# Fourth conv tile ahead of keys and queries, and 64-row score products on two halves of the array

## The chip, the cores and the metric

The kernel runs on one core of a Trainium2 chip. The metric is the device time of one execution in microseconds (us). Its engines work side by side, each through its own list of instructions in order: TensorE (PE: matrix products; PEld: loading the stationary operand), VectorE (DVE), ScalarE (ACT), GpSimd (POOL) and SyncE (SP, which here only issues transfers). They wait for one another through semaphores. A program (the tile framework's scheduler) turns the code below into those lists: it takes the order of the code as a priority, but puts an instruction later or earlier where it expects an operand or a buffer to be late.

## The reference

Two layers, each on 512 positions of 1024 features: a feed-forward block, a mixer and a second feed-forward block. The change is in the mixer.

```python
h = rms_norm(x, mix_norm[l])
a, g, q, k, v = jnp.split(h @ w_in[l], splits, axis=-1)
conv_out = conv_module(a, g, conv_w[l], conv_b[l], conv_norm[l])   # GLU, causal depthwise conv (31 taps), norm, swish
q = rms_norm(q.reshape(B, S, H, 2, d).transpose(0, 2, 3, 1, 4), q_norm[l])   # H = 4 heads, 2 maps, d = 64
k = rms_norm(k.reshape(B, S, H, 2, d).transpose(0, 2, 3, 1, 4), k_norm[l])
...
s = jnp.einsum("bhmqd,bhmkd->bhmqk", qi, k) * scale + bias      # blocks of 128 queries, causal
p = jax.nn.softmax(s, axis=-1)
a = p[:, :, 0] - lam * p[:, :, 1]                               # difference of the head's two maps
o = jnp.einsum("bhqk,bhkd->bhqd", a, v)
...
x = x + jnp.concatenate([conv_out, diff_out], axis=-1) @ w_out[l]
```

## The kernel before

Activations are kept with features on the 128 partitions. The large products are made three times over, with a high and a low part of each operand (`mm3`, L158 to L164). The high part of a weight chunk comes from ScalarE (L97), the low part from VectorE or GpSimd (L98); `chunk` (L100) loads and splits one, and its `eng` says who makes the low part. Chunks live in rings of four or five buffers, so a new one waits for an old one to be used up.

`mixer` (L530) does, in the order of its code from L777 on:

- `conv_in(c)` (L537): for conv tile c of four, the products for the gated linear unit (48 matmuls, `ps_pair`), then VectorE and ScalarE make `u` (L557 to L563). The low parts for c = 3 come from GpSimd. The first two tiles are worked together, with the row norms among them.
- `project(which, pair)` (L574): keys (1) and queries (0), two of the four position tiles a call, 48 matmuls (L585 to L587), then the sums of squares (L593, L594), the power on GpSimd (`rsqrt`, L209) and the scaled `qn` (L600). `to_features` (L620) transposes `qn` on TensorE (L624); ScalarE copies the result to `kt`, or twice to `qz`: `qz[:, m]` holds the queries of map m with zeros in the other map's 64 rows, because the factor `gq[:, m]` is zero there (L512 to L517).
- `project_values(j)` (L606): V for one position tile, 24 matmuls (`ps_v`).
- `conv_taps(c, n)` (L646): the 31 taps of a tile. GpSimd adds the first n, with products made by ScalarE (L656, L657); VectorE does the others in one PSUM bank (tag `y`, one buffer, L664 to L669). `POOL_TAPS` gives n for each tile: all 31 for tile 0, none for 1 and 2, ten for 3. For tile 3 VectorE adds GpSimd's sum at the end (L673). `conv_finish` (L678) norms over the four tiles and writes `ch`, `cl` (L687, L688).
- `attend(n)` (L767): step n of 16 (4 query blocks from the last, 4 heads each, so heads of width 512, 384, 256 and 128). `softmaxes` (L694) makes the score product of each map (L703) into a bank of tag `sc` (map 0) or `po` (map 1), two banks each. VectorE adds the bias and takes the minimum (L707, here all signs are turned), ScalarE makes the exponential and its sum (L711). VectorE then makes a factor `c` (L714, L716) and the difference of the maps `e0` (L717). Two steps later `keys_first` (L720) transposes it, a step after that `values` (L729) multiplies by V (L733), and `block_out` (L756) transposes the block's output (L760) and splits it.
- The output projection (L804 to L814): half 0 takes the conv tiles, then half 1 the attention blocks 2 and 3, then 0 and 1; its banks are `sc` and `po` too.

The conv, key and query products also use the banks `sc`, `po` and `mm` in turn (`turn_tag`, L309), so a conv tile that is moved moves them all by one.

Of the kernel before, what the change touches and what calls it, by code (L numbers as in the profile page):

```python
# [11 lines left out]
F32 = mybir.dt.float32  # L12
F32R = mybir.dt.float32r
I32 = mybir.dt.int32
AF = mybir.ActivationFunctionType
ALU = mybir.AluOpType
AX = mybir.AxisListType

P = 128
DEPTH = 2  # L20
SEQ = 512
# [8 lines left out]
TAPS = 31  # L30
# [18 lines left out]

POOL_TAPS = (TAPS, 0, 0, 10)  # L50

# [16 lines left out]
def trunk(ctx: ExitStack, tc: tile.TileContext, xt, par, lamv, relb, onehot,  # L68
# [133 lines left out]
    def col(l, name, i=0):  # L202
        c = _AT[name] + i
        return pars[l][:, c : c + 1]
# [291 lines left out]
    def make_scalars():  # L496
        for l in range(DEPTH):
# [13 lines left out]
            nlam.append(nl)  # L511
            g = const.tile([P, 2], F32, tag=f"gq{l}", name=f"gq{l}")  # L512
            G.memset(g, 0.0)
            for m in range(2):
                d = slice(m * HD, (m + 1) * HD)
                G.tensor_tensor(g[d, m : m + 1], col(l, "q_norm")[d], col(l, "k_norm")[d], op=ALU.mult)
            G.tensor_scalar(g, g, -math.sqrt(HD), None, op0=ALU.mult)  # L517
# [12 lines left out]
    def mixer(l, pr, after):  # L530
        with tc.tile_pool(name="mix", bufs=1) as mp, tc.tile_pool(name="mt", bufs=2) as mt:
# [36 lines left out]

            qz = mp.tile([P, 2, HEADS, SEQ], F32, tag="qz", name="qz")
            kt = mp.tile([P, HEADS, SEQ], F32, tag="kt", name="kt")  # L570
# [49 lines left out]
            def to_features(which, pair):  # L620
                for j in (2 * pair, 2 * pair + 1):
# [5 lines left out]
                    if which == 1:  # L627
                        S.activation(kt[:, :, t], pt, AF.Copy)
                    else:
                        for m in range(2):  # L630
                            S.activation(qz[:, m, :, t], pt, AF.Copy, scale=gq[l][:, m : m + 1])

# [61 lines left out]
            def softmaxes(i, h):  # L694
# [7 lines left out]
                for m in range(2):  # L702
                    T.matmul(scs[m], qz[:, m, h, tq], kt[:, h, :W], start=True, stop=True)  # L703

# [10 lines left out]
                c2 = small.tile([P, 1], F32, tag="c2", name="c2")  # L715
                V.tensor_scalar(c2, r2, nlam[l], sm[:, 0, h : h + 1], op0=ALU.mult, op1=ALU.mult)  # L716
                V.scalar_tensor_tensor(e0, scs[1], c2, e0, op0=ALU.mult, op1=ALU.add)  # L717
# [58 lines left out]

            for c in range(CT - 1):  # L777
                conv_in(c)
# [6 lines left out]
            to_features(0, 0)  # L785
            conv_in(CT - 1)
            to_features(0, 1)
            bias = mp.tile([P, HEADS, SEQ], F32, tag="bias", name="bias")
            nc.sync.dma_start(bias, skew[0])
            row["bias"] = bias  # L790

            for n in range(2):
                attend(n)
                project_values(NT - 1 - 2 * n)
                project_values(NT - 2 - 2 * n)
            for c in range(CT):
# [124 lines left out]
```

## Time and profile before

| what | value |
|---|---|
| median of 3 runs | 1797.92 us (1797.81 to 1798.19) |
| the profiled execution | 1798.12 us |
| its span in the profile | 1796.4 us |
| busy: TensorE, its loads, VectorE | 1785.4, 1590.2, 1215.1 us |
| busy: ScalarE, GpSimd | 895.9, 654.5 us |
| start of the first and the last score pass in the first layer | 460.0 and 511.6 us from the span's start |

A row of a group gives line, engine, operation, result and operands, shapes and count, then busy time and mean length of one in ns, then idle time of the engine ahead of it. A row of the timeline gives start and length in us, engine, line, operation, operands and count; in brackets stands how long the engine sat idle before it and what ended that. A matmul's record begins while the one before is still streaming, so lengths overlap, and the time that one takes from the engine is read from start to start. A row of a stretch gives its bounds, its length and the busy time with instruction count of PE, PEld, DVE, ACT and POOL, then the granted TensorE clock, the DMA share and GB/s.

### The profile page before, as it was taken

The numbers are of one execution on the slowest core, as the hardware profiler recorded it, in microseconds if no ns is written. First come the engines' busy times: TensorE is split into PE (matmuls) and PEld (weight loads), VectorE is DVE, ScalarE is ACT, GpSimd is POOL, SyncE is SP. The second block draws the span as 40 slices with busy tenths as digits, with TensorE's granted clock in tenths as the row PEclk, the third lists the DMA queues.
The fourth block names the chain that finished last, engine by engine and source line by source line (L and its number), as shares of the span: only waits on it lengthen the run. The fifth ranks groups of instructions, "written<-read, shape, count | busy, mean of one in ns | idle before, by whom it ended". The sixth has DMA issues, their size and how long they took to land.

```text
span 1796.4 us, 28354 instructions
## 1 busy us (share of the span) xinstructions
PE 1785.4 (99%) x10845; PEld 1590.2 (89%) x10845; DVE 1215.1 (68%) x1862; ACT 895.9 (50%) x1482; POOL 654.5 (36%) x460
## 2 busy tenths in 40 slices
PE   9999999999999999999999999999999999999999
PEld 6899899888778899899888998998887888998997
DVE  7977477569867867477476764765788587673762
ACT  5555255445854446256433543654558354552651
POOL 4242232269843133132112312412797331322420
PEclk9999999999999999999999999999999999999999
DMA  7466476333212366466333664663231133664651
GB/s 242 104 167 197 100 178 187 107 105 94 71 48 83 94 164 179 115 170 184 110 94 95 171 169 115 179 182 118 71 113 52 48 106 89 168 178 112 178 151 59
DMA packets 111721, 231.24 MB, mean 129 GB/s; under 512 B 12151, under 2 KB 33414, under 8 KB 111584
## 3 DMA queue, kind: packets, MB, share of 16 engines
q1 hardware_dynamic: 91488, 191.93, 33.2%
q0 software_dynamic: 19808, 37.33, 12.7%
q8 instruction: 85, 1.39, 0.3%
q14 instruction: 52, 0.43, 0.1%
q10 hardware_dynamic: 288, 0.16, 0.0%
HBM read 227.26 MB, written 3.42 MB: 128 GB/s over the span
## 4 chain that ended last, share of the span: by engine, by line
PE 95%; DVE 2%; issue 1%; ACT 1%; ACTq 0%; DVEq 0%
PE ps_pair L373 38%; PE ps_d L160 9%; PE ps_d L164 9%; PE ps_d L163 9%; PE ps_pair L164 5%; PE ps_pair L163 5%; PE ps_pair L160 5%; PE ps_pair L585 2%; PE ps_pair L586 2%; PE ps_pair L587 2%; PE ps_out L163 1%; PE ps_out L160 1%; PE ps_sc L703 1%; PE ps_out L164 1%; DVE actl L258 1%; PE ps_v L617 1%
## 5 line engine op out<-in xcount | busy, mean ns | idle before, releaser
L97 ACT ACTIVATE whi<-wraw 128x512 fp32r<-128x512 f32 (+2 forms) x600 | 466.2, 801 | 616.4 <-PE ps_pair L373 225.7
L98 DVE TENSOR_TENSOR wlo<-wraw,whi 128x512 fp32r<-128x512 f32 (+2 forms) x556 | 527.4, 971 | 210.1 <-ACT whi L97 205.0
L373 PE MATMUL ps_pair<-acth,wlo 128*128 128x256 f32 x1088 | 307.9, 283 | 0.0
L373 PE MATMUL ps_pair<-actl,whi 128*128 128x256 f32 x1088 | 307.9, 283 | 0.0
L373 PE MATMUL ps_pair<-acth,whi 128*128 128x256 f32 x1088 | 307.9, 283 | 0.0
L163 PE MATMUL ps_d<-hl,whi 128*128 128x512 f32 x704 | 273.9, 389 | 0.0
L164 PE MATMUL ps_d<-hh,wlo 128*128 128x512 f32 x704 | 273.0, 389 | 0.0
L160 PE MATMUL ps_d<-hh,whi 128*128 128x512 f32 x704 | 268.4, 389 | 0.0
L373 PE MATMUL ps_pair<-th,wlo 128*128 128x256 f32 x816 | 230.9, 283 | 0.0
L373 PE MATMUL ps_pair<-tl,whi 128*128 128x256 f32 x816 | 230.8, 283 | 0.0
L373 PE MATMUL ps_pair<-th,whi 128*128 128x256 f32 x816 | 230.8, 283 | 0.0
L143 POOL TENSOR_TENSOR wraw<-wraw 128x512 f32<-128x512 f32 x68 | 104.1, 1531 | 345.5 <-DMA wraw<-in_gu 293.0
L138 POOL DMA_DIRECT2D wraw<-in_gu x68 | 82.0, 1206 | 384.1 <-DMA wraw<-in_gu 228.0
L373 PEld LDWEIGHTS ps_pair<-actl,whi 128*128 128x128 f32 x1088 | 208.9, 192 | 0.3
L373 PEld LDWEIGHTS ps_pair<-acth,whi 128*128 128x128 f32 x1088 | 208.9, 192 | 0.3
L373 PEld LDWEIGHTS ps_pair<-acth,wlo 128*128 128x128 f32 x1088 | 208.9, 192 | 0.0
L469 DVE SCALAR_TENSOR_TENSOR x<-ps_d,x 128x512 f32<-128x512 f32 x96 | 64.7, 688 | 179.1 <-PE ps_d L164 178.8
L164 PE MATMUL ps_pair<-acth,wlo 128*128 128x512 f32 x448 | 174.5, 391 | 1.1 <-DVE wlo L98 1.1
L163 PE MATMUL ps_pair<-actl,whi 128*128 128x512 f32 x448 | 174.6, 391 | 0.6 <-DVE actl L258 0.3
L160 PE MATMUL ps_pair<-acth,whi 128*128 128x512 f32 x448 | 174.5, 394 | 0.2
L373 PEld LDWEIGHTS ps_pair<-tl,whi 128*128 128x128 f32 x816 | 156.5, 192 | 0.7
L373 PEld LDWEIGHTS ps_pair<-th,whi 128*128 128x128 f32 x816 | 156.5, 192 | 0.6
(174 smaller groups left out, 3268.8 us busy)
## 6 DMA issues: line engine op xcount, KB each, us to landing
wraw<-in_gu SPq DMA_DIRECT2D x208, 256.0 KB, 4.0
wraw<-in_gu SPq DMA_DIRECT2D x104, 512.0 KB, 3.7
wraw<-in_gu POOLq DMA_DIRECT2D x68, 512.0 KB, 5.8
wraw<-in_wqkv SPq DMA_DIRECT2D x24, 512.0 KB, 3.6
wraw<-in_dn SPq DMA_DIRECT2D x84, 128.0 KB, 3.0
wraw<-in_dn SPq DMA_DIRECT2D x32, 256.0 KB, 3.1
wraw<-in_wag SPq DMA_DIRECT2D x16, 512.0 KB, 3.6
wraw<-in_wout SPq DMA_DIRECT2D x16, 512.0 KB, 3.6
```

What stands on the lines that cost most here:

```text
L97: S.activation(hi, raw, AF.Copy)
L98: (eng or V).tensor_tensor(out=lo, in0=raw, in1=f32(hi), op=ALU.subtract)
L138: nc.gpsimd.dma_start(two.rearrange("p (b c) -> p b c", b=2), u[:, h[0]].unsqueeze(1).broadcast_to([P, 2, 512]), accum_op=ALU.add)
L143: G.tensor_tensor(more[:, h[0]], two[:, h[1]], whole[:, h[0]], op=ALU.add)
L160: first = T.matmul(ps, wh, xh, start=start, stop=False)
L163: T.matmul(ps, wh, xl, start=False, stop=False)
L164: T.matmul(ps, wl, xh, start=False, stop=stop)
L373: mm = T.matmul(ps, l, r, start=first and i == j == 0, stop=False, skip_group_check=True)
L469: V.scalar_tensor_tensor(x[:, m, :], ps, 0.5, x[:, m, :], op0=ALU.mult, op1=ALU.add)
L585: T.matmul(ps[n], xh[:, t], wh, start=k == 0, stop=False)
L586: T.matmul(ps[n], xh[:, t], wl, start=False, stop=False)
L587: T.matmul(ps[n], xl[:, t], wh, start=False, stop=k == KT - 1)
```

## The change

The query copy with zeros goes: `qt` holds the queries once, with one factor for all 128 rows, and each score product takes the 64 rows of its map from `qt` and `kt`. So map 0 lies on the first half of TensorE's rows and map 1 on the second. The fourth conv tile is projected with the other three, ahead of keys and queries. Two V tiles stand ahead of the last `to_features`, and the first two steps of `attend` among the other two. GpSimd takes 6 taps of the fourth tile instead of 10. The factor `c` is made by another instruction with the same operands.

```diff
-POOL_TAPS = (TAPS, 0, 0, 10)
+POOL_TAPS = (TAPS, 0, 0, 6)
...
-            g = const.tile([P, 2], F32, tag=f"gq{l}", name=f"gq{l}")
-            G.memset(g, 0.0)
-            for m in range(2):
-                d = slice(m * HD, (m + 1) * HD)
-                G.tensor_tensor(g[d, m : m + 1], col(l, "q_norm")[d], col(l, "k_norm")[d], op=ALU.mult)
+            g = const.tile([P, 1], F32, tag=f"gq{l}", name=f"gq{l}")
+            G.tensor_tensor(g, col(l, "q_norm"), col(l, "k_norm"), op=ALU.mult)
             G.tensor_scalar(g, g, -math.sqrt(HD), None, op0=ALU.mult)
...
-            qz = mp.tile([P, 2, HEADS, SEQ], F32, tag="qz", name="qz")
+            qt = mp.tile([P, HEADS, SEQ], F32, tag="qt", name="qt")
...
-                        for m in range(2):
-                            S.activation(qz[:, m, :, t], pt, AF.Copy, scale=gq[l][:, m : m + 1])
+                        S.activation(qt[:, :, t], pt, AF.Copy, scale=gq[l])
...
                 for m in range(2):
-                    T.matmul(scs[m], qz[:, m, h, tq], kt[:, h, :W], start=True, stop=True)
+                    half = slice(m * HD, (m + 1) * HD)
+                    T.matmul(scs[m], qt[half, h, tq], kt[half, h, :W], start=True, stop=True)
...
-                V.tensor_scalar(c2, r2, nlam[l], sm[:, 0, h : h + 1], op0=ALU.mult, op1=ALU.mult)
+                V.scalar_tensor_tensor(c2, r2, nlam[l], sm[:, 0, h : h + 1], op0=ALU.mult, op1=ALU.mult)
...
-            for c in range(CT - 1):
+            for c in range(CT):
                 conv_in(c)
             project(1, 0)
             project(1, 1)
...
             project(0, 1)
             to_features(0, 0)
-            conv_in(CT - 1)
-            to_features(0, 1)
             bias = mp.tile([P, HEADS, SEQ], F32, tag="bias", name="bias")
             nc.sync.dma_start(bias, skew[0])
             row["bias"] = bias

-            for n in range(2):
-                attend(n)
-                project_values(NT - 1 - 2 * n)
-                project_values(NT - 2 - 2 * n)
+            project_values(NT - 1)
+            project_values(NT - 2)
+            to_features(0, 1)
+            attend(0)
+            project_values(NT - 3)
+            attend(1)
+            project_values(NT - 4)
             for c in range(CT):
                 conv_taps(c, POOL_TAPS[c])
```

## The prediction

> **What bounds the kernel now.** I read the page first: span, busy shares and the chain that ended last. Then the busy time in stretches of the first layer's attention, then the score products by shape, then the order of single instructions on TensorE and VectorE.
>
> ```profile
> span 1796.4 us, 28354 instructions
> PE 95%; DVE 2%; issue 1%; ACT 1%; ACTq 0%; DVEq 0%
> 474.00:490.30 16.30, 15.87 (x83) 11.02 (x81) 11.69 (x39) 14.23 (x34) 13.81 (x10) 1.00 0.45 131
> 490.30:503.62 13.32, 11.77 (x80) 9.72 (x80) 13.08 (x52) 10.68 (x35) 7.84 (x8) 1.00 0.00 0
> 503.62:515.20 11.58, 11.32 (x60) 8.74 (x61) 11.58 (x35) 9.01 (x26) 2.90 (x5) 1.00 0.01 1
> ```
>
> The chain that ended last lies on TensorE for 95% of the span. So what counts is TensorE work taken away or added and TensorE waits opened or closed. The columns of the stretches are length, then busy time of TensorE, its weight loads, VectorE, ScalarE and GpSimd, then granted clock (1.00 throughout), DMA share and GB/s. In the first stretch TensorE is nearly full. In the second VectorE is (13.08 of 13.32 us) and TensorE is not, in the third both are. The change lies in this stage, which stands twice in the program, once a layer. There TensorE and VectorE are nearly balanced, so work taken from TensorE is only worth what VectorE lets through.
>
> **What the score products cost.** A product of head and map goes through TensorE as two passes. One layer has 16 heads' worth (4 query blocks of 4 heads, here h0 to h15) with two maps (m0, m1), so 64 passes:
>
> ```profile
> L703 PE MATMUL ps_sc<-kt,qz 128*128 128x512 f32 x16 | 7.5, 592 | 0.0
> L703 PE MATMUL ps_sc<-kt,qz 128*128 128x384 f32 x16 | 6.2, 487 | 0.0
> L703 PE MATMUL ps_sc<-kt,qz 128*128 128x256 f32 x16 | 4.6, 382 | 0.0
> ...
> 474.36 0.39 PE L617 MATMUL ps_v<-whi,actl 128*128 128x512 f32 x1
> 474.59 1.88 PE L703 MATMUL ps_sc<-kt,qz 128*128 128x512 f32 x4
> 476.30 0.60 PE L724 MATMUL ps_at<-ident,e 128*128 128x128 f32 x4
> 476.74 2.53 PE L703 MATMUL ps_sc<-kt,qz 128*128 128x512 f32 x6
> ...
> 481.73 1.05 PE L733 MATMUL ps_o<-vv,at 128*128 128x128 f32 x8
> 482.62 0.81 PE L703 MATMUL ps_sc<-kt,qz 128*128 128x384 f32 x2
> ```
>
> Durations overlap in the pipeline, so I take starts. Four 512-wide passes take 476.30 - 474.59 = 1.71 us, 0.427 each; scaled with width, 16 x 0.427 x (1 + 3/4 + 1/2 + 1/4) = 17.1 us a layer. Transposes take 0.44/4 = 0.11 us, value passes 0.89/8 = 0.11 us.
>
> **Edit 1, half-height products.** Each product keeps its columns and its two passes; only its rows are halved. It gains if passes on the two halves run side by side, which needs an m0 and an m1 next to each other in TensorE's order, both ready. The order of the changed program has this at the start of a layer (h0m0 h0m1 h1m0 h1m1). After that come h2m0 h3m0 h4m0 h5m0, then single m1 products with transposes and value passes between, in 16 groups a layer. Only eight passes stand in alternation. If the second pass of one half runs beside the first of the other, 8 spans become 5, a gain of 3 x 0.427 = 1.3 us. Four joints between narrower products give at most 0.5 more. Bounds on TensorE: 0 to -1.8 us a layer; I take -1.3. Of that only what someone waits for reaches the end: in this start a full product takes 0.85 us where VectorE, by the rows below, needs 0.61 for it, so three gaps of 0.24 close, -0.7 us.
>
> The opposite bound is the cost of going between full and partial array. The trace has that in the bias product (33 rows), beside the full-height product of the row factors:
>
> ```profile
> 42.58 0.39 PE L164 MATMUL ps_pair<-acth,wlo 128*128 128x512 f32 x1
> 42.90 0.09 PEld L486 LDWEIGHTS ps_bias<-oneh,relb 33*4 33x4 f32 x2 [0.35 <-issue]
> 42.90 1.02 PE L486 MATMUL ps_bias<-oneh,relb 33*4 33x512 f32 x2
> 43.85 0.19 PEld L160 LDWEIGHTS ps_pair<-acth,whi 128*128 128x128 f32 x1 [0.86 <-issue]
> 43.85 0.50 PE L160 MATMUL ps_pair<-acth,whi 128*128 128x512 f32 x1
> 44.18 0.39 PE L163 MATMUL ps_pair<-actl,whi 128*128 128x512 f32 x1
> ...
> 371.92 0.40 PE L164 MATMUL ps_pair<-acth,wlo 128*128 128x512 f32 x1
> 372.16 1.02 PE L240 MATMUL ps_spread<-diag,ones 128*128 128x512 f32 x2
> 372.61 0.79 PE L160 MATMUL ps_pair<-acth,whi 128*128 128x512 f32 x1
> 373.24 0.40 PE L163 MATMUL ps_pair<-actl,whi 128*128 128x512 f32 x1
> ```
>
> From the L164 ahead to the second matmul behind, the partial product takes 44.18 - 42.58 = 1.60 us and the full one, with as many passes of 512 columns, 373.24 - 371.92 = 1.32. The weights of the partial one were loaded only at 42.90, when the product before was ending, and the load behind it likewise. So in and out cost 0.28 us together. Sixteen groups would be 4.5 us a layer if all lay on TensorE's path; the other bound is 0, where TensorE waits anyway. Thirteen groups (3.6 us) lie before the output projection, where the sum below leaves TensorE waiting: I take 0 for them. Three lie inside the projection, where it has work: 3 x 0.28 = 0.8 us.
>
> [...]
>
> **Edit 2, the order.** In the old program h0 and h1 are scored inside the V projection, so their softmax runs on VectorE while TensorE has V products. In the new one the fourth conv tile stands ahead of K and Q, and all four V tiles stand ahead of the first score. The work ahead is the same, so the first score starts 8 x 0.427 = 3.4 us earlier than 474.59, at 471.2. But all 16 heads then follow with nothing to fill in. VectorE:
>
> ```profile
> 452.99 7.09 DVE L669 SCALAR_TENSOR_TENSOR ps_y<-u,par,ps_y 128x512 f32<-128x512 f32 x9
> ...
> 464.23 0.70 DVE L707 CUSTOM_DVE_ANT_0 ps_sc<-ps_sc,bias 128x512 f32<-128x512 f32 x1
> 464.84 0.75 DVE L669 SCALAR_TENSOR_TENSOR ps_y<-u,par,ps_y 128x512 f32<-128x512 f32 x1
> ...
> 466.29 0.27 DVE L716 TENSOR_SCALAR c<-r,nlam,sums 128x1 f32<-128x1 f32 x1
> 466.47 0.74 DVE L669 SCALAR_TENSOR_TENSOR ps_y<-u,par,ps_y 128x512 f32<-128x512 f32 x1
> 467.13 0.74 DVE L717 SCALAR_TENSOR_TENSOR e<-ps_sc,c,e 128x512 f32<-128x512 f32 x1
> 467.79 0.15 DVE L714 RECIPROCAL r<-sums 128x1 f32<-128x1 f32 x1
> 467.86 0.73 DVE L669 SCALAR_TENSOR_TENSOR ps_y<-u,par,ps_y 128x512 f32<-128x512 f32 x1
> ...
> 475.65 0.69 DVE L707 CUSTOM_DVE_ANT_0 e<-ps_sc,bias 128x512 f32<-128x512 f32 x1 [2.52 <-PE ps_sc L703]
> ...
> 512.27 0.74 DVE L688 SCALAR_TENSOR_TENSOR actl<-u,ghalf,acth 128x512 fp32r<-128x512 f32 x1
> ```
>
> A 512-wide head costs VectorE 2 x 0.61 (464.84 - 464.23) + 0.07 (467.86 - 467.79) + 0.18 (466.47 - 466.29) + 0.66 (467.79 - 467.13) = 2.13 us; by width I estimate 1.3 for 256 and 0.9 for 128. From its first product of h2 (475.65) to the low part of the fourth conv tile (512.27) it needs 36.6 us, waits included, with 12 whole heads between (two of 512, four each of 384 and 256, two of 128). In the new order the same instruction stands behind 11 whole heads (four, four, three, none): +2 x 2.13 - 1.3 - 2 x 0.9 = +1.2 us. The new form of c is an instruction like
>
> ```profile
> L740 DVE SCALAR_TENSOR_TENSOR se<-sums x8: 132/154/164, 480.0 to 1398.7; 128x4 f32<-128x4 f32 x8
> ```
>
> 0.15 for 0.27 us, 11 x 0.12 = -1.3. So again 36.5 us, from 471.2 + 0.9 (first product) = 472.1: the fourth tile's low part starts at 508.6 instead of 512.27. VectorE has four more taps at 7.09/9 = 0.79 us, 3.2 us, but they come before the first score. All taps end near 469 by the old rows, so about 3 us of slack hide them; without it they would be 3.2 us on the path.
>
> TensorE's first output product stands in the new order behind the transposes of block 2, whose input VectorE writes 1.2 us (0.60 for itself, the rest small ones) before that fourth tile: start about 507.4. TensorE's own work from 471.2 to there (26 score products 16.6, 34 transposes 3.7, 68 value passes 7.5, row sums, spread and output transposes 2.3) is 30.1 us, to 501.3. With all thirteen switches it would be 504.9, still before 507.4: VectorE sets this time.
>
> ```profile
> 503.62 0.50 PE L160 MATMUL ps_out<-acth,whi 128*128 128x512 f32 x1 [1.26 <-ACT acth L687]
> ...
> 531.31 0.28 PE L160 MATMUL ps_out<-acth,whi 128*128 128x256 f32 x1
> ```
>
> In the old kernel that first half of the projection lasts from 503.62 to 531.31, 27.7 us, with some 1.5 us of waits for conv tiles. In the new one all tiles are nearly there: 96 x 0.227 = 21.8, left-over heads 3.6, switches 0.8 and 0.5 of waits, 26.7 us, to 534.1. That is 534.1 - 531.3 = **+2.8 us a layer**.
>
> **The rest.** GpSimd loses four tap additions, ScalarE four tap products and four of its eight copies of queries a layer:
>
> ```profile
> 486.47 1.27 POOL L657 TENSOR_TENSOR yp<-yp,prod 128x512 f32<-128x512 f32 x1 [0.20 <-ACT prod L656]
> L631 ACT ACTIVATE qz<-ps_pair,gq 128x512 f32<-128x512 f32 x8 | 4.8, 690 | 3.1 <-PE ps_pair L624 3.1
> ```
>
> The last tap would end at 487.7 - 4 x 1.27 = 482.7. The add that waits for it now stands on VectorE after three heads, at about 472.1 + 3 x 2.13 + 4 products of h3 to h5 (2.2) + waits 1.5 = 482.2. So this gain is used up, and if GpSimd is later every microsecond stalls all softmax behind it: 0 to +2 us, I take +0.3. The four copies lie beside V products: 0 now, a gain of some 2.4 us if TensorE had to wait for them. The moved weight loads keep their count; the bias load passes ahead of all key loads on the SP queue, whose splits start over ten microseconds later than before: 0.
>
> **The sum.** A layer: +2.8 (order, with the switches in the projection) + 0.3 (late tap) - 0.7 (first products side by side) = +2.4; two layers **+4.8 us** on 1798.12 us, the profiled execution (span 1796.4 and 1.7 around it; the median of the runs is 1797.92): **1802.9 us**. Bounds a layer: downwards VectorE's waits gone (some 3.2 us between its rows from 475.65 to 512.27), no switch paid (0.8), no late tap (0.3) and the joints gained (0.5), 2.4 - 4.8 = -2.4; upwards a tap late by 2 us (+1.7), the other 13 switches on the path (+3.6) and nothing side by side (+0.7), +8.4. For two layers 1793 to 1815.
>
> **The rivals.**
> 1. *The halves run side by side and the conv part, three heads earlier in VectorE's order, closes the waits* (the other side). For it: all conv tiles lie ready when the projection starts, and both engines have waits in the old stretches. Against it: groups of one map, and a VectorE that is full from 490 on. By the lower bound 1793. It decides if VectorE's gaps between first score and fourth conv tile come to under 1 us. Chance 0.17. Complete halving of the 17.1 us on the path would be 8.5 us less in each layer, 1781; the order keeps the maps apart, so I hold 0.03 for that.
> 2. *Nothing measurable.* V and conv change places, the scores cost what they did, and the waits that open at the start of the scores are those that close in the projection: 1798, within 3.6 us (0.2%, about what a measurement of this kernel can tell from no change). For it: VectorE needs 36.5 against 36.6 us. Chance 0.2.
> 3. *Switches and the late tap on the path*: 2.4 + 1.7 + 3.6 = +7.7 a layer, 1813. It decides if VectorE waits for scores whose weights were loaded only when the product before had ended. Against it: TensorE has 2.5 us to spare with all of them. Chance 0.1.
>
> My forecast, VectorE setting the start of the projection some 4 us later than before, has 0.5, most of it above 1801.5, where slower by 0.2% begins. So slower 0.1 + 0.45 = 0.55, same 0.2 + 0.05 = 0.25, faster 0.17 + 0.03 = 0.2. The range is 1792 to 1811; out of it lie halving, the upper half of rival 3 and little else. The forecast's own is 1800 to 1807.
>
> **What would show it.** Right: in the stretch from first score to first output product TensorE is busy markedly below the old share and VectorE near full, V products end before the first score, and the output product starts about 4 us later. Partial products show weight loads not overlapped with what is before. Wrong: score passes of m0 and m1 with the same start in many groups, or a TensorE wait inside K, Q or V for a low part from GpSimd. That I count as 0:
>
> ```profile
> 376.23 2.41 POOL L98 TENSOR_TENSOR wlo<-wraw,whi 128x1024 fp32r<-128x1024 f32 x1 [9.39 <-ACT whi L97]
> ```
>
> At 2.41 us a split and 1.27 a tap its new order, followed through by hand from 376.23, has the last V split ready near 454.4, and its first use on TensorE falls near 457.3; the others have 2 to 5 us too.

## The result, and the profile after

The changed kernel takes 1823.6 us (median of 4 runs, 1819.1 to 1824.9) against 1797.9 for the kernel before (1797.7 to 1798.2): ratio 1.0139, 95% interval 1.0126 to 1.0151, so +25.7 us where +4.8 was forecast. The profiled execution took 1822.8 us, and the rows below are of that one.

Three lines of its page: span, granted TensorE clock in 40 slices, and the chain that ended last.

```profile
span 1820.8 us, 28323 instructions
PEclk9999999999999999999999999999997999999999
PE 95%; DVE 3%; issue 1%; DVEq 0%
```

The chain reads much as before. What is new is a 7 among the nines of the clock line, in the attention of the second layer. Busy time by stretch shows what it is (length, then busy time of TensorE, weight loads, VectorE, ScalarE, GpSimd, then granted clock, DMA share, GB/s). Four rows follow the second layer's attention, the last belongs to the first layer:

```profile
1369.50:1375.70 6.20, 5.91 (x18) 2.00 (x18) 4.93 (x17) 6.20 (x15) 6.20 (x4) 1.00 0.29 91
1375.70:1396.20 20.50, 20.50 (x58) 12.31 (x58) 12.43 (x35) 8.27 (x23) 6.65 (x5) 0.50 0.24 75
1396.20:1413.20 17.00, 15.53 (x84) 10.34 (x84) 14.51 (x44) 12.80 (x36) 5.63 (x6) 1.00 0.00 1
1413.20:1420.10 6.90, 6.67 (x23) 5.35 (x24) 6.33 (x23) 4.57 (x14) 1.21 (x2) 0.51 0.00 0
508.70:512.10 3.40, 3.31 (x13) 2.73 (x13) 3.37 (x14) 2.45 (x7) 0.00 (x0) 0.50 0.02 5
```

For 20.5 us the clock is at 0.50. TensorE is full there and VectorE, which should set the pace, works only 12.43 us. Two shorter falls follow the later heads, one in each layer. Read more finely, the falls last 3.41, 20.48 and 6.83 us: one, six and two times 3.41. They start at 508.70, 1375.69 and 1413.24, and the distances are whole multiples of it too, 254 and 11 times 3.413. Half of their 30.7 us is lost where TensorE has work, at most 15.4 us.

The landmarks on TensorE in the first layer (the second row is the weight load of the fifth score product), and two of the second:

```profile
471.21 7.18 PE L700 MATMUL ps_sc<-kt,qt 64*128 64x512 f32 x18
473.12 0.29 PEld L700 LDWEIGHTS ps_sc<-kt,qt 64*128 64x128 f32 x2 [0.76 <-DVE mn L704]
511.14 0.77 PE L160 MATMUL ps_out<-acth,whi 128*128 128x512 f32 x1
561.48 0.40 PE L160 MATMUL ps_pair<-acth,whi 128*128 128x512 f32 x1
1369.54 8.01 PE L700 MATMUL ps_sc<-kt,qt 64*128 64x512 f32 x18
1418.20 0.77 PE L160 MATMUL ps_out<-acth,whi 128*128 128x512 f32 x1
```

The first score starts at 471.21 (forecast 471.2). The first output product starts 39.9 us later (forecast 36.2), and in the second layer 48.7 us later. The row at 561.48 is the first product after the mixer; in the kernel before it was this one:

```profile
554.77 0.40 PE L160 MATMUL ps_pair<-acth,whi 128*128 128x512 f32 x1
```

So the first layer loses 6.7 us, and most of the rest is lost in the second.

GpSimd and VectorE in the first layer, from the timeline:

```profile
473.56 6.98 POOL L98 TENSOR_TENSOR wlo<-wraw,whi 128x1024 fp32r<-128x1024 f32 x3
480.51 1.26 POOL L653 TENSOR_TENSOR yp<-yp,prod 128x512 f32<-128x512 f32 x1
...
472.37 0.69 DVE L704 CUSTOM_DVE_ANT_0 e<-ps_sc,bias 128x512 f32<-128x512 f32 x1 [2.16 <-PE ps_sc L700]
...
477.32 0.94 DVE L713 SCALAR_TENSOR_TENSOR c<-r,nlam,sums 128x1 f32<-128x1 f32 x1
...
478.96 1.61 DVE L737 SCALAR_TENSOR_TENSOR se<-sums 128x4 f32<-128x4 f32 x1
480.49 0.69 DVE L704 CUSTOM_DVE_ANT_0 ps_sc<-ps_sc,bias 128x512 f32<-128x512 f32 x1
...
482.72 0.21 DVE L713 SCALAR_TENSOR_TENSOR c<-r,nlam,sums 128x1 f32<-128x1 f32 x1
...
483.91 0.67 DVE L669 TENSOR_TENSOR u<-ps_y,yp 128x512 f32<-128x512 f32 x1
...
509.99 0.74 DVE L684 SCALAR_TENSOR_TENSOR actl<-u,ghalf,acth 128x512 fp32r<-128x512 f32 x1
```

An operation on one number a row takes 0.94 us, one on four 1.61. GpSimd's three splits of 2.33 us end near 475.9, 478.2 and 480.5; c ends at 478.26 and se at 480.57. Both stand still until the running GpSimd instruction ends, while a 512-wide product that starts beside the last tap takes its usual 0.69.

### The profile page after: what moved, and what is told of

Its sections match the earlier page's. It is cut to its first block, busy times and chain, and to the rows that moved or that the text cites. A ratio compares the mean times of both kernels' runs of the same rounds, so it can differ in the third digit from the quotient of the medians.

```text
span 1820.8 us, 28323 instructions
## 1 busy us (share of the span) xinstructions
PE 1807.7 (99%) x10845; PEld 1596.3 (88%) x10845; DVE 1235.3 (68%) x1870; ACT 888.4 (49%) x1466; POOL 649.8 (36%) x448
## 3 DMA queue, kind: packets, MB, share of 16 engines
HBM read 227.26 MB, written 3.42 MB: 127 GB/s over the span
## 4 chain that ended last, share of the span: by engine, by line
PE 95%; DVE 3%; issue 1%; DVEq 0%
PE ps_pair L373 38%; PE ps_d L164 9%; PE ps_d L163 9%; PE ps_d L160 9%; PE ps_pair L163 5%; PE ps_pair L164 5%; PE ps_pair L160 5%; PE ps_pair L583 2%; PE ps_pair L582 2%; PE ps_pair L584 2%; PE ps_out L160 1%; PE ps_out L164 1%; PE ps_out L163 1%; PE ps_sc L700 1%; PE ps_v L612 1%; PE ps_v L613 1%
## 5 line engine op out<-in xcount | busy, mean ns | idle before, releaser
L98 DVE TENSOR_TENSOR wlo<-wraw,whi 128x512 fp32r<-128x512 f32 (+2 forms) x556 | 534.6, 983 | 200.1 <-ACT whi L97 194.9
L143 POOL TENSOR_TENSOR wraw<-wraw 128x512 f32<-128x512 f32 x68 | 113.0, 1661 | 347.1 <-DMA wraw<-in_gu 299.4
```

The source lines that it names most:

```text
L98: (eng or V).tensor_tensor(out=lo, in0=raw, in1=f32(hi), op=ALU.subtract)
L143: G.tensor_tensor(more[:, h[0]], two[:, h[1]], whole[:, h[0]], op=ALU.add)
```

## The experiments

The change has four parts: the order of the stages (O), six taps instead of ten on GpSimd (T), the new form of c (C), half-height products with queries kept once (H). The table gathers the runs that combine them. Each was timed beside the kernel before.

```
parts       us       ratio and 95% interval
none        1797.9
C           1799.0   1.0005 (0.9995 to 1.0014)
H           1800.1   1.0010 (1.0001 to 1.0019)
O           1803.5   1.0031 (1.0020 to 1.0043)
O H         1804.9   1.0038 (1.0025 to 1.0052)
O T         1806.5   1.0045 (1.0028 to 1.0062)
O T C       1811.9   1.0079 (1.0064 to 1.0094)
O T H       1812.0   1.0078 (1.0063 to 1.0093)
O T C H     1823.6   1.0139 (1.0126 to 1.0151)
```

One way through it: O +5.6, T +3.0, C +5.4, H +11.7, together 25.7. But C alone costs 1.2 and on top of O, T and H 11.6; H alone costs 2.0, on top of O 1.4, of O and T 5.5, of O, T and C 11.7. The parts do not add up; they share something.

**Full height again** (O T C):

```
-    T.matmul(scs[m], qt[half, h, tq], kt[half, h, :W], ...)
+    T.matmul(scs[m], qz[:, m, h, tq], kt[:, h, :W], ...)      # qz zero-padded, as before
```

> The changed kernel with its score products at full height again, queries zero-padded for each map as before; order of the stages, taps and the form of c as changed. Theory A, half-height passes count as less work for what grants TensorE its clock, and this took the clock from 1.00 to 0.50 for 3.4 us in the first layer and 27 us in the second: here the clock is 1.00 in both attention stretches, and the time falls from 1823.6 to 1800 to 1807 us. Rival B, the new order leaves TensorE waiting for VectorE and those waits take the clock down: the stretches at 0.50 stay, 1815 to 1825 us.

Measured: 1811.9 us (1810.0 to 1816.5), mean clock 1.00 in the profiled execution and 0.998 in the three others. The second layer:

```profile
1368.00:1374.20 6.20, 6.16 (x15) 2.38 (x13) 4.32 (x13) 6.20 (x14) 6.20 (x4) 1.00 0.30 85
1374.20:1395.00 20.80, 18.85 (x106) 13.52 (x106) 20.00 (x55) 13.56 (x38) 11.79 (x10) 1.00 0.27 77
```

At the same place, with the same order, TensorE now gets 106 instructions done in 20.8 us where it got 58, and VectorE is busy for 20.00. So the long fall belongs to the half-height products. But the time came out above the 1800 to 1807 expected, and the clock can't be the whole reason: the profiled execution took 1810.0 us, 12 more than the kernel before, without any fall. So order, taps and c lose time at full clock too. One place for it shows in this trace, ahead of the output projection. (`ov` is the output of query block 2, which VectorE writes and TensorE then transposes.)

```profile
508.20 0.68 DVE L748 TENSOR_TENSOR ov<-ps_o,rs_y 128x512 f32<-128x512 f32 x1
509.27 0.73 DVE L688 SCALAR_TENSOR_TENSOR actl<-u,ghalf,acth 128x512 fp32r<-128x512 f32 x1
...
508.94 0.66 PE L760 MATMUL ps_o<-ident,ov 128*128 128x128 f32 x4 [1.51 <-DVE ov L748]
...
510.65 0.71 PE L733 MATMUL ps_o<-vv,at 128*128 128x128 f32 x4 [0.61 <-ACT at L726]
511.12 0.47 PE L160 MATMUL ps_out<-acth,whi 128*128 128x512 f32 x1
```

VectorE writes `ov` 1.07 us ahead of the fourth conv tile (1.2 forecast). But the first output product doesn't follow at once: TensorE still does the transposes and another head's products, with a wait for ScalarE between, and starts it 2.92 us behind the start of `ov`.

**The old form of c** (O T H), and **both** (O T):

```
-    V.scalar_tensor_tensor(c2, r2, nlam[l], sm[:, 0, h : h + 1], op0=ALU.mult, op1=ALU.mult)
+    V.tensor_scalar(c2, r2, nlam[l], sm[:, 0, h : h + 1], op0=ALU.mult, op1=ALU.mult)
```

> The changed kernel with c in its old form (tensor with two scalars) only. Theory lock: the new form of c, with both its inputs in SBUF, stands still until GpSimd's running instruction ends (0.94, 1.02 us where GpSimd is busy, 0.21 where it is not); in the old form every c is back at 0.26 to 0.27, VectorE's way from the first score to the first output product is some 1.5 us shorter in a layer, and the time falls by 2 to 4 us, to 1819 to 1822, if the stretches at half clock stay. Rival: c is not on the path, within 1 us of 1823.6. Theory A: the mean clock stays under 1.00; rival B the same.

> The changed kernel with full-height score products and the old form of c: of the change only the order and six taps instead of ten remain. Theory A with the forecast's account of the order (+2.4 us a layer, of which 0.8 was for switches that are gone and -0.7 for halves side by side): clock 1.00, 1799 to 1804 us. Rival B (order takes the clock down): 1815 us or more with stretches at 0.50.

Measured: 1812.0 and 1806.5 us, mean clock 0.994 and 0.997. The first gain, 11.6 us, was much more than the 2 to 4 expected. The second lies above its 1799 to 1804, and here neither theory holds in its first form: all products are of full height, and the clock still falls, late in the attention:

```profile
503.20:506.61 3.41, 1.77 (x11) 1.15 (x11) 3.41 (x13) 3.41 (x10) 0.00 (x0) 1.00 0.02 5
506.61:513.44 6.83, 6.30 (x21) 5.04 (x20) 4.01 (x18) 2.38 (x11) 0.00 (x0) 0.50 0.00 0
```

In the 3.41 us ahead of that fall TensorE had work for 1.77 us by its records, which overlap; VectorE was full. VectorE's first product and the low part of the fourth conv tile in the same run:

```profile
471.52 0.69 DVE L707 CUSTOM_DVE_ANT_0 e<-ps_sc,bias 128x512 f32<-128x512 f32 x1 [1.95 <-PE ps_sc L703]
...
507.28 0.74 DVE L688 SCALAR_TENSOR_TENSOR actl<-u,ghalf,acth 128x512 fp32r<-128x512 f32 x1
```

Those 35.8 us are what the forecast took as 36.5. The first output product, though, starts only at 509.30, 2.0 us behind the fourth tile, where the forecast had it 1.2 ahead, and the first product after the mixer at 559.48, 4.7 us later than in the kernel before. Now look at the stretch ahead of the long fall in the changed kernel, all engines and then TensorE's instructions that touch it, by shape:

```profile
1372.28:1375.69 3.41, 3.12 (x8) 1.01 (x8) 3.34 (x13) 3.41 (x12) 3.41 (x2) 1.00 0.34 130
```

```profile
L700 PE MATMUL ps_sc<-kt,qt 64*128 64x512 f32 x4 | 2.8, 750 | 0.1
L700 PE MATMUL ps_sc<-kt,qt 64*128 64x384 f32 x4 | 1.8, 535 | 0.2
```

TensorE looks busy (3.12 of 3.41), but with half-height passes alone. This suggests one rule for both: the work in a stretch of 3.41 us counts, and half-height work counts for less, in my sums for half. Here is the lowest stretch of the kernel before (counted back in steps of 3.413 from its one fall, at 1795.03, where its TensorE work is done), which kept its clock, and the one ahead of the changed kernel's fall in the first layer:

```profile
501.36:504.77 3.41, 2.06 (x13) 1.47 (x13) 3.41 (x11) 2.82 (x11) 3.33 (x4) 1.00 0.02 5
505.29:508.70 3.41, 2.02 (x11) 1.31 (x10) 3.41 (x11) 2.99 (x11) 1.21 (x2) 1.00 0.00 0
```

By the records, which overlap, TensorE is busy alike in both (2.06 and 2.02 us). By passes it is not. I summed it over the stretches of every profile, each pass at the 0.427 us that 512 columns take (half of that, 0.213, for single-pass products, which take 0.227 from start to start); this is an estimate, good to about 0.1 us. In the stretch at 1372.28 four passes of 0.427 and four of 0.320 us, less what lies outside, come to 2.40 us, counted half 1.20. In 17 profiles (all but the second probe below) 24 of the 25 falls in and around the attention follow stretches counted at 0 to 1.24 us, the other one at 1.35; the lowest stretches that kept the clock come to 1.25 and 1.26, **and the kernel before stands at 1.33** in both layers, while the changed kernel's row at 505.29 counts 0.85. Counted in full, the stretch of 2.40 us fell while others of 1.33 us did not. The clock comes back after stretches counted at 2.56 us or more, and not after any up to 2.51. At half clock a pass takes nearly twice as long (an output product of 512 columns 0.42 to 0.43 us from start to start instead of 0.227). Halved, those figures are the passes of 1.28 and 1.25 us at full clock: by these counts one limit in work, about 1.25 us of full-clock passes in a stretch, serves for the fall and for the return.

**c alone, half height alone:**

> The kernel before with the new form of c and nothing else. Theory lock: c stands still until GpSimd's running instruction ends wherever GpSimd is busy (0.4 to 2.4 us in two to four of the 16 heads of a layer, against 0.27); the old order has GpSimd busy nearly all the time from 474 to 486 us, where VectorE still has gaps, so 0.5 to 3 us a layer, 1799 to 1804 us, and in a busy place single records of c of 1 us or more. Rival (the forecast's term for it): c is 0.12 us shorter in every head, 1795 to 1798 us, no record over 0.3 us.

> The kernel before with half-height score products and queries kept once, and nothing else changed: old order, ten taps, old form of c. Theory A: in the old order the half-height products of the first two heads stand among V products of full height, but those after them follow as close as in the changed kernel, so the clock falls in at least one of the layers and the mean clock is under 1.00: 1800 to 1820 us. Rival B (waits of the new order alone): clock 1.00 and 1794 to 1799 us.

Measured: 1799.0 and 1800.1 us, clock 1.00 in all runs of both. For c, the instructions of its line, before and with the new form (min, median and max in ns):

```profile
L716 DVE TENSOR_SCALAR c<-r,nlam,sums x32: 258/268/274, 466.3 to 1404.8; 128x1 f32<-128x1 f32 x32
```

```profile
L716 DVE SCALAR_TENSOR_TENSOR c<-r,nlam,sums x32: 200/219/1550, 466.1 to 1405.8; 128x1 f32<-128x1 f32 x32
```

The median is shorter, as the forecast had it, but the longest is 1.55 us: the gain and the stalls nearly cancel where VectorE has room, and the 1.2 us in all can't be told from no change. On order and taps at full height (O T C) five of its records a layer are stalled, for 0.33 to 1.38 us, 2.9 us more than at 0.20 each. For half height the expectation that the clock falls in the old order was wrong: its lowest stretch is counted at 1.48 us.

**Order alone, and order with half height** (ten taps, old c):

> The new order alone: full-height products, old form of c, ten taps of the fourth conv tile on GpSimd as before (with six it measured 1806.5 us). Theory order: what costs time is that all 16 heads follow one another with no V products between, so it is still 1803 to 1810 us with a stretch at half clock in the last part of the attention. Rival taps: the four taps given to VectorE are the cost; then 1797 to 1801 us.

> The changed kernel with the old form of c and ten taps: new order and half-height products alone. With full height it measured 1803.5 us, clock 1.00, its lowest stretch at 1.8 us of work. Theory A: the half-height passes of the third to fifth head count half and are near 1.25 us in their stretch, so at least in some executions the clock falls there: mean clock under 1.00 and 1804 to 1814 us. Rival (half height costs nothing by itself, only together with c and the taps): 1801 to 1804 us, clock 1.00.

Measured: 1803.5 us, clock 1.00 in all six runs, and 1804.9, clock 1.00 in four of five. In the order alone the stretch at half clock that I expected isn't there. The first output product starts 35.2 us after the first score, with half height 35.9, so half height costs 0.7 a layer there; I had expected more. In the first layer the first score also comes 0.66 us earlier with it (470.43 instead of 471.09), so the first output product starts at nearly the same time. By the table the price of half height comes with the taps and c, which thin TensorE's work out further: at full height it is busy for 42.59 of the 44.80 us from 471.2 to 516 with the order alone, 40.65 with the taps and 38.26 with both.

```profile
506.24 0.51 PE L160 MATMUL ps_out<-acth,whi 128*128 128x512 f32 x1 [0.45 <-ACT acth L687]
...
514.93 0.74 DVE L688 SCALAR_TENSOR_TENSOR actl<-u,ghalf,acth 128x512 fp32r<-128x512 f32 x1
...
557.42 0.40 PE L160 MATMUL ps_pair<-acth,whi 128*128 128x512 f32 x1
```

These rows are of the order alone: first output product, low part of the fourth conv tile, first product after the mixer. The last gives 557.42 - 554.77 = +2.65 us in the first layer.

**Do the halves run side by side, and what counts for the clock?** Two probes. In the first, 24 score products in a row ahead of the first softmax, which nobody reads, on one half in the first layer and on both in turn in the second:

```
+    for n in range(24):
+        mm = T.matmul(pb[n % 2], qt[cut(n), 0, :P], kt[cut(n), 0, :], start=True, stop=True)
```

> The kernel before with half-height products, and in each layer 24 more score products of 128x512 in a row, which nobody reads, ahead of the first softmax: in the first layer all on the lower half of the rows, in the second on the lower and upper half in turn. They add work, the time itself says nothing. Theory A, half-height passes count as half the work for what grants the clock: in the first layer TensorE has no gap for 20 us (48 passes of 0.43 us) and yet the clock falls to 0.50 within 7 us; in the second the halves run side by side, 24 products take 11 to 13 us, and the clock stays 1.00. Rival: only gaps count, the clock is 1.00 in both. If halves do not run side by side in the second, both take 20 us.

```profile
457.56 17.86 PE L795 MATMUL ps_probe<-kt,qt 64*128 64x512 f32 x41
...
1370.43 10.57 PE L795 MATMUL ps_probe<-kt,qt 64*128 64x512 f32 x48
1380.83 1.02 PE L700 MATMUL ps_sc<-kt,qt 64*128 64x512 f32 x4
```

In turn, 48 passes take 10.4 us, 0.217 each instead of 0.427: the halves do run side by side. On one half they take the old time (20 us), and the clock stayed 1.00 against my expectation. (One fall came in the second layer, behind the probe: TensorE waited 5.69 us there for VectorE, and one whole stretch had no work at all.) Counted half, a packed row is 1.7 us in 3.41, above the limit, so the simple form of the theory falls and the one with a threshold stands. The second probe has gaps: each product waits until VectorE has read the one before, with 64 rows in the first layer and 128 in the second.

> The changed kernel with the old form of c and, between the V products and the third head, 18 more products of 128x512 in a row in each layer, each waiting until VectorE has read the one before (nobody uses them); in the first layer they have 64 rows, in the second 128. The time itself says nothing. A product should take 0.85 us of work in every 1.7 us. Theory A (work of half height counts half, and under about 1.25 us in a stretch of 3.41 us the clock is halved): 0.85 us counted in the first layer, so the clock goes to 0.50 within two stretches of the first lonely products and stays there, and 1.7 us in the second, so it stays 1.00 there until the products end. Rival (only TensorE's gaps count): the same clock in both layers, 1.00 or 0.50.

```profile
487.96:491.37 3.41, 2.63 (x10) 0.92 (x8) 1.42 (x3) 0.00 (x0) 0.88 (x1) 1.00 0.67 227
491.40:525.50 34.10, 24.92 (x26) 6.11 (x26) 13.55 (x20) 6.04 (x9) 4.86 (x4) 0.50 0.01 2
...
1433.45:1436.86 3.41, 2.20 (x14) 1.53 (x13) 2.19 (x3) 0.60 (x1) 3.41 (x2) 1.00 0.71 175
1436.86:1440.28 3.42, 2.64 (x11) 1.35 (x11) 1.89 (x3) 0.00 (x0) 1.35 (x2) 1.00 0.84 254
1440.28:1443.69 3.41, 2.63 (x6) 0.78 (x5) 1.38 (x2) 0.87 (x2) 1.57 (x2) 1.00 0.08 31
```

With 64 rows a stretch busy for 2.63 us took the clock down, and it stayed at 0.50 for 41 us, of which the row shows 34.1. With 128 rows three stretches busy for 2.20 to 2.64 us kept it. It then fell there too, after a stretch with one product (0.85 us counted), and stayed down for 27.3 us, which was not expected. In this run two falls came after stretches counted at 1.33 and 1.37 us and one at 1.51, so the limit by my count lies between about 1.25 and 1.5, not at a sharp figure. That half height counts for less than full height is shown by this; that it counts exactly half is not.

**Filling the waits**, in the kernel with O and T: a single-pass product of ones ahead of each score product of the last two blocks.

> The kernel with the new order and six taps, full-height products and old c (measured 1806.5 us, 5.1 us lost to half clock in its profile), and ahead of every score product of the last two query blocks one single-pass product of 512 columns of ones into the same bank, which nobody reads. Theory: the clock falls when TensorE has been at work for less than about half of a 3.41 us stretch (1.58 and 1.77 us of busy in the stretches ahead of the two falls, 2.15 and more where it did not fall), so with 0.23 us more work twice a head the clock is 1.00 throughout, and the time falls by 1 to 4 us, to 1802.5 to 1805.5. Rival: the falls have another cause and stay, and the added 3.7 us a layer of TensorE work makes it slower, 1807 to 1812 us.

Measured: 1807.9 us (ratio 1.0055, 1.0040 to 1.0070), mean clock 0.999 against 0.997: above the 1802.5 to 1805.5 expected. The falls shrink from three times 3.41 us to one, but the filler costs as much as the clock gives. What the clock alone is worth in that kernel stays open.

**V tiles back between the first heads.** Three runs put three V tiles behind the first two heads, with the fourth conv tile still ahead of keys and queries. In all three, TensorE also keeps every V product and the first two heads' score products in the order of the code (`keep_in_program_order`), which the changed kernel does not ask for:

```
     project_values(NT - 1)
     to_features(0, 1)
     attend(0)
     attend(1)
+    project_values(NT - 2)
+    project_values(NT - 3)
+    project_values(NT - 4)
```

> As the kernel with the new order, six taps, full-height products and old c (1806.5 us), but with three of the four V tiles (72 products, 16.4 us of TensorE) put behind the first two heads, so that their softmax runs beside V products as in the kernel before; the fourth conv tile stays ahead of keys and queries. Theory order: the loss is the missing V work beside the first heads; with it back the last part of the attention has no stretch at half clock and the time is 1795 to 1800 us. Rival: the conv tile ahead of keys and queries costs by itself (GpSimd and VectorE later); then 1803 us or more.

> The changed kernel with the old form of c (1812.0 us) and three V tiles behind the first two heads. Theory order and A: the half-height passes of the third to sixth head no longer stand alone in a 3.41 us stretch, TensorE is never under 1.25 us of work (half-height counted half) in one, clock 1.00, 1794 to 1801 us. Rival: half-height products themselves cost the 5.5 us between the kernel with full height and this one, whatever the order: 1801 to 1806 us.

> The kernel with V tiles behind the first two heads, full height, old c, and ten taps of the fourth conv tile on GpSimd. Against the kernel before only the fourth conv tile's place ahead of keys and queries and two V tiles' places are changed. Theory order: 1794 to 1799 us, clock 1.00. Rival (the place of the conv tile costs): 1801 us or more.

Measured: 1821.3, 1821.2 and 1824.4 us (ratios 1.0132, 1.0135 and 1.0144, intervals within 1.0109 to 1.0160). All three expectations missed by over 20 us. TensorE's waits in the first one, ahead of the transposes of the queries:

```profile
449.53 1.22 PE L624 MATMUL ps_pair<-ident,qn 128*128 128x128 f32 x8 [2.14 <-DVE qn L600]
458.34 1.94 PE L624 MATMUL ps_pair<-ident,qn 128*128 128x128 f32 x8 [2.10 <-DVE qn L600]
```

The conv tile or V tiles between a projection and its transposes hide VectorE's normalization (qn): in the kernel before TensorE has no wait ahead of these transposes. In the changed order only the V tiles are left for that: in the changed kernel the scheduler begins V products at 447.53, ahead of the queries' last transposes at 453.43, and TensorE has no wait there either. The three runs both move V tiles and forbid that, and which of the two opens the waits was not separated. The clock also falls behind these waits, before the first score product at 461.36: in the first run it is 0.77 from 456.59 to 460.00, where TensorE is busy for 1.66 us, and 0.50 from there to 465. So these runs say nothing on what the conv tile's place costs by itself.

**Pairs in the old order:** half height, the two maps of every head next to each other on TensorE.

> The kernel before with half-height products, and the two maps of a head kept next to each other in TensorE's order in all 16 heads (map 1 first). Theory: in adjacent pairs the passes of the two halves start together and a 512-wide head takes 0.95 us and not 1.71; then TensorE's work falls by 7 us a layer, but from 490 us on VectorE sets the pace, so only the stretch from the last V product to there gains: 1792 to 1797 us, clock 1.00. Rival: a pair has to wait for the second bank, which comes free only after the softmax, so VectorE gets its first map later in each head: 1800 to 1808 us.

Measured: 1808.1 us (1.0057, 1.0040 to 1.0073). The rival came true: score products wait 8.2 us in all (10 times) for VectorE's last reading (`e`) of the second bank, and the clock falls after this stretch, in which VectorE is full and TensorE works half the time, but in its last 3.42 us for only 0.74:

```profile
501.65:508.48 6.83, 3.53 (x25) 2.65 (x25) 6.69 (x21) 6.48 (x20) 3.65 (x4) 1.00 0.01 2
```

Side by side gained nothing here, where VectorE sets the pace.

**VectorE's load and its stalls**, in the kernel before. First, the last product of two of the four conv tiles moved to GpSimd; then tanh of the conv tiles written to an accumulation bank, so that the product that reads it has only one input in main on-chip memory:

```
-    th = mt.tile([P, SEQ], F32, tag="gl", name="th", bufs=1)
+    th = bank("y", "th")
```

> The kernel before with the last product of two of the four conv tiles (one VectorE instruction of 0.68 us each) done on GpSimd in two instructions of 1.27 us each. Theory: VectorE sets the pace from 490 us to the fourth conv tile (13.08 of 13.32 us busy), so 1 to 1.4 us less of it a layer shows as 0.5 to 2.5 us: 1795.5 to 1797.5 us. Rival: the four GpSimd instructions come too late for the output projection, or hold VectorE up where both read two operands from the same memory: 1799 to 1804 us.

> The kernel before with the tanh of the conv tiles written to an accumulation bank instead of the main on-chip memory, nothing else. Theory lock: a VectorE instruction waits for GpSimd's running one only if both its inputs lie in the main memory; the first conv tile's product of tanh and tile, 1.30 us in the kernel before with GpSimd at work beside it, then takes 0.7 us, the first output product starts 0.4 to 0.6 us earlier in each layer, and the time is 1796.5 to 1797.5 us. Rival 1: the instruction stalls for another reason and still takes 1.2 us or more, 1797.5 to 1798.5. Rival 2: the one bank makes tanh of the next tile wait for VectorE, and later tiles come later: 1798 to 1800 us.

Measured: 1799.0 us (1.0006, 0.9997 to 1.0014), a miss: the first conv tile opens the projection, not VectorE's total, and the moved tiles came later (low part of the fourth at 514.3 instead of 512.3). And **1796.7 us** (0.9994, 0.9985 to 1.0003) against 1798.0, ten of its eleven runs below all fifteen of the kernel before. The instruction before and in that run:

```profile
L686 DVE SCALAR_TENSOR_TENSOR yp<-th,yp x2: 1296/1297/1298, 501.5 to 1392.3; 128x512 f32<-128x512 f32 x2
```

```profile
L686 DVE SCALAR_TENSOR_TENSOR yp<-th,yp x2: 680/680/681, 501.3 to 1391.4; 128x512 f32<-128x512 f32 x2
```

GpSimd is at work beside it in both (500.12 to 503.76 and 499.88 to 503.08). With one input moved the stall is gone. It is the only version here whose median is under the kernel before, by 1.3 us, less than its interval can tell from none.

## Why the prediction was wrong

- **Right: where the first score and VectorE's work lie.** The first score came at 471.21 (471.2). VectorE's way from its first product to the fourth conv tile, forecast as 36.5 us, took 35.8 with order and taps, 37.6 in the changed kernel (472.37 to 509.99). Both halves of the projection take 50.3 us in the changed kernel (511.14 to 561.48) against 26.7 forecast for the first and 23.5 that the second took before.
- **The order: near, in part by luck.** It was forecast at +2.8 us a layer, 0.8 of it for switches, so +2.0 at full height. The order alone measures +2.65 in the first layer and 5.6 us in all, but it goes another way than was said: with ten taps its fourth tile comes only at 514.9 and the projection starts at 506.2, before it. With the six taps that the forecast was for, the first layer ends 4.7 us later, not 2.0.
- **Right: the first pairs, the late tap, no wait in K, Q and V.** The first four products take 1.9 us (471.21 to 473.12) and not 3.4, a gain of 1.5 for 1.3 forecast. The 0.7 that was to reach the end is not seen: half height on the order alone loses 0.7 a layer up to the projection. The add behind the last tap (483.91) found it done (481.8), and cost nothing.
- **Wrong in sign: the new form of c.** It was taken at 0.15 us for 0.27, a gain of 1.3 us a layer, from eight records of a like instruction, of which only two had met a GpSimd instruction, 0.14 us ahead of its end. In the new order with six taps it costs 5.4 us in all at full height and 11.6 at half height. The trace of before did show the stall: product of tanh and tile 1.30 us at 501.51, beside GpSimd's products of 512 columns, 0.68 at 507.24, where GpSimd does nothing, and also 0.68 at 504.45, beside its power (`rs_y`).
- **The first step that failed: every TensorE duration at clock 1.00.** "Granted clock (1.00 throughout)" was read off the old stretches and carried into a kernel with less TensorE work in the same time. The forecast itself had TensorE done at 501.3 and waiting to 507.4 (at its own 0.427 us the 26 score products come to 15.8 us and not 16.6, so it had 0.8 us still less to do); it priced those waits, half-height work and added stalls each for itself and never asked what they do together to the clock. At most 15.4 us of the profiled run were lost to it. Full height in the same kernel brings back 11.7 us, the old c 11.6, both 17.1.
- **The second: the start of the first output product.** It was put where VectorE writes the input of block 2's transposes, with nothing for what TensorE does between: 507.4, 1.2 us ahead of the fourth tile. At full height and full clock it started 2.92 us behind the start of that input and 1.85 behind the tile (511.12 against 509.27); in the changed kernel 2.36 and 1.15 (511.14 against 509.99), partly at half clock. So the loss without any fall, 12 us in the profiled run of full height, comes from the order with this start, the taps and c. How it splits between them was measured only by the steps of the table.
- **Switches: small, as taken.** Half height on the order alone costs 0.7 us a layer up to the projection; 13 x 0.28 us, the bound, would be 3.6. Whether it is switches is not shown.
- **The taps: not free.** VectorE's own time for them was hidden, as forecast: with order and taps it still waits 1.95 us for its first score. Yet with the order they cost +3.0 us. The output projection starts 3.1 us later in the first layer than with ten taps (509.30 against 506.24), and clock falls of 6.83 and 3.41 us come with them. How much of the 3.0 is clock was not separated.
- **The rivals.** Rival 1's mechanism is real (0.217 us a pass instead of 0.427 in the first probe), but in the changed kernel only eight 512-wide passes a layer, and a few narrower ones, use it. Rival 3 had the right sign and the wrong cause.

The falls in the changed kernel's attention go to 0.50, for 3.41, 20.48 and 6.83 us. One fall followed a stretch without any work (in the first probe, 1386.88 to 1390.29 us). The others followed stretches in which TensorE had work, busy for 3.12 of 3.41 us by its records ahead of the long one: thin work is enough. The stalls seen here are of VectorE instructions with both inputs in main on-chip memory, beside a GpSimd instruction: 1.30 us that became 0.68 with one input moved, c with 0.94 instead of 0.20 to 0.22, se with 1.61 instead of 0.15. What the two engines share there is not shown.

## What to carry to other kernels

Before work is taken from TensorE where another engine sets the pace, sum what is left of it in each stretch of 3.41 us, half-height work at less than full, here at half: by that count this kernel stood at 1.33 us, and the edits took single stretches to 0.85 to 1.20, where the clock halved. When you place a product behind an engine's last input, price also what stands between them in the queue. Price a VectorE instruction with two inputs in main on-chip memory by the GpSimd instruction beside it (c up to 1.55 us), not by its own median (0.22). A change of several edits, each nearly free alone (C 1.2, H 2.0 us), can cost far more together, so take it apart in combinations and not one by one.

## What was not expected of the hardware

Half-height work held the clock down once it was down: at half speed TensorE was full for six stretches (20.48 us) and still counted at most 2.5 us in the five after which the clock stayed down, which is 1.25 us at full clock, while the full-height kernel (O T) came back after one or two. The clock differed between the layers of one program: the same passes counted 1.26 us in one stretch of the first layer and kept it, 1.20 in the second and lost it, as the stretches fall otherwise on the instructions; this may be why the changed kernel's runs spread by 5.8 us and those of the kernel before by 0.5, but it is not shown. And a packed row of half-height passes on one half (20 us) kept the clock at 1.00, though nothing in it is faster than at full height.
